# A decoder block in fp32 on one Trainium2 core: output projection as seven block products, second feed-forward begun by a hand order with six chunks

## The chip, the cores and the metric

The kernel runs on one core of a Trainium2 chip. The time is the device time of one execution in microseconds (us); the kernel before took 1117.46 us, the median of 3 runs (1116.97 to 1117.51). Engines are named as in the profile: PE (TensorE), DVE (VectorE), ACT (ScalarE), POOL (GpSimd) and SP (SyncE, which here only issues transfers).

## What is computed

One decoder block on 512 tokens with 1024 features: feed-forward, token mixing, feed-forward, each between two norms. The change touches the end of the token mixing (the output projection, its norm and residual) and the first chunks of the second feed-forward. The reference, cut to that:

```python
def hybrid_mixer(u, ...):
    ...
    merged = jax.nn.sigmoid(g_lru) * (y_lru @ w_proj_lru) + jax.nn.sigmoid(g_attn) * (y_attn @ w_proj_attn)
    return merged @ w_out

def reference(x, ...):
    ...
        m = hybrid_mixer(rms_norm(h, mix_pre_g[l]), ...)
        h = h + rms_norm(m, mix_post_g[l])
        f = swiglu(rms_norm(h, ffn2_pre_g[l]), ffn2_w_gu[l], ffn2_w_down[l])
        h = h + MACARON_SCALE * rms_norm(f, ffn2_post_g[l])
```

`swiglu` projects to 2 x 2816 columns, multiplies silu of one half with the other, and projects back.

## The kernel before

**Products.** Every fp32 product is made of three matmuls (`mm3`, L157 to L160) on operands that are split into a high and a low part: high by high, high by low, low by high. A weight half of 128 x 1024 numbers is loaded by SP (`wload`, L102, tile `wraw`), cast to its high part on ACT (`wround`, L112, tile `w`), and its low part is the difference, on DVE (`wsplit`, L120). `worder` lists all weight halves in the order in which they are used; `wget` hands out the next one and keeps the split some halves ahead.

**Stages.** In the order of time: the first feed-forward; the mixing's input projections; the left-gate stage (tiles `glg`, `glp`, eight chunks, 527 to 639 us in the trace), into which the attention of the last head groups is woven (`at20b`, `at30b` and so on: scores of group 2 and 3, block 0); the right-gate stage (`gag`, `gap`, 640 to 727 us), which ends with the merged features `mg`, split into high and low; the output projection (`token_out`, L449, tiles `woo`); and the second feed-forward: `first_four` (L238, four column chunks `f2f`, each in two halves of 256 tokens), four more whole chunks (`f2g`), and then the rest in pairs as block products (`paired`, tiles `f2X` and others).

**Attention's queries.** A group's rotated queries pass through memory: SP stores them (`q_halves`, L960) and reads them back in another layout in four transfers (`qt`, L965). `at20b` is the first user of `qt2`, `at30b` of `qt3`. The sums of attention's blocks (`at20s` and others) run on POOL.

**Output projection.** For each of 4 token tiles and 2 column halves a bank adds up 8 chunks. Seven of the chunks are held back, so that a tile is finished at a time. Its epilogue (`boundary`, L481) follows at once on the other engines: squares on ACT (`half`, L502), gains on DVE (L506), an inverse root on POOL (L203), the residual (L529), a second norm (L534 to L542, tile `b2un`). Then PE transposes the tile (`b2ntp`, L218), and ACT and DVE split it (`u3h` L222, `u3l` L223).

**What sets the order.** In all these stages a scheduler decides the order of instructions on each engine from the program's order and its own costs; blocks under `manual_schedule` keep the order that is written. Each engine then runs its list in order. Transfers issued by SP go to one queue (q1 in the profile), those by POOL to another (q0). The kernel before already has sums of weights in memory for the down projections: SP copies (`wsum`, L393), and POOL adds to the copy (an accumulating transfer, L395).

Of the kernel before, what the change touches and what calls it, by code (L numbers as in the profile page):

```python
# [8 lines left out]
F32 = mybir.dt.float32  # L9
# [33 lines left out]
def hybrid_block_kernel(ctx, tc, x, xt, g1, w_first, gains, gu1, gs1, dn1, w_x, w_gate, w_q, w_k, w_v, w_gl, w_ga, w_pl, w_pa,  # L43
# [12 lines left out]
    def bank(name):  # L56
        return psum.tile([P, 512], F32, name=name, tag="bank")
# [154 lines left out]
    def to_features(un, t, u, name, raw=None):  # L212
        keep = []
        for half in range(2):
            b = bank(f"{name}tp{t}{half}")
            for i in range(4):
                k = 4 * half + i
                PE.transpose(out=b[:, i * P:(i + 1) * P], in_=un[:, k * P:(k + 1) * P], identity=ident)  # L218
            bv = b.rearrange("p (k t) -> p k t", k=4)
            ts_ = slice(t * P, (t + 1) * P)  # L220
            uh, ul = u[0][half][:, :, ts_], u[1][half][:, :, ts_]
            A.copy(uh, bv)  # L222
            V.tensor_tensor(out=ul, in0=bv, in1=uh.bitcast(F32), op=ALU.subtract)  # L223
            if raw is not None:
                keep.append((raw[half][:, :, ts_], bv))
        for z, bv in keep:
            A.copy(z, bv)

    def feat_chunk(b, w, u, tok):
        wh, wl = w  # L230
# [7 lines left out]
    def first_four(u, name, done):  # L238
# [14 lines left out]
    def gate_up(u, name, first, fast, then, rs=None):  # L253
        ps = []

        def slot(j):
# [21 lines left out]
            if i % 2 == 1:  # L278
                tail(i // 2, bs[i - 1], b)

        first(u, f"{name}f", done)
        run = paired(fast, name, slot, then(ps))
        for j in range(2, JSTD[name]):
            if j == JSTD[name] - 1:
                next(run)
# [13 lines left out]
    def paired(fast, name, slot, then):  # L299
# [78 lines left out]

        for k in range(3):
            load(k)  # L380
        sums(0)
        parts(0, 1)
        parts(0, 2)
# [62 lines left out]
            add(n - 1, 21)  # L446
            finish(n - 1)

    def token_out(chunk, n, finish, name, tail_n):  # L449
        half, epilogue, _ = finish  # L450
        banks = {}

        def block(t, c, w, i):
            ph, pl = chunks[c]
            ts_ = slice(t * P, (t + 1) * P)
            if (t, i) not in banks:
                banks[t, i] = bank(f"{name}o{t}{i}")
            ns = slice(i * 512, (i + 1) * 512)
            mm3(banks[t, i], ph[:, c % 4, ts_], pl[:, c % 4, ts_], w[0][:, ns], w[1][:, ns], c == 0, c == n - 1)

        chunks = {}
        tail = []
        for c in range(n):
            w = wget()
            chunks[c] = chunk(c)
            if c < n - tail_n:
                for t in range(NT):
                    for i in range(2):
                        block(t, c, w, i)
                tick()  # L470
            else:
                tail.append((c, w))
        for t in range(NT):
            for i in range(2):
                for c, w in tail:
                    block(t, c, w, i)
            for i in range(2):
                half(t, i, banks[t, i])
            start(epilogue(t))
            tick()  # L480

    def boundary(src, dst, g_post, g_pre, u, scale, name, raw=None, then=None):
        rhs = []

        def residual():
# [4 lines left out]
                rhs.append(rh)  # L490

        cols = (slice(0, 512), slice(512, 1024))
        sq, parts, late = {}, {}, {}

        def half(t, i, z, sign=1.0, o=None):
            if t not in sq:
                sq[t], parts[t] = sm(f"{name}ps{t}", 2), [None, None]
# [4 lines left out]
            A.activation(t4(f"{name}sq{t}{i}")[:, :512], z, AF.Square, scale=1.0 / 32.0, accum_out=sq[t][:, i:i + 1])  # L502
            parts[t][i] = o

            def gain():
                V.scalar_tensor_tensor(out=o, in0=z, scalar=sign * scale, in1=g_post[:, cols[i]], op0=ALU.mult,  # L506
                                       op1=ALU.mult)

            if i == 0:
                gain()  # L510
            else:
                late[t] = gain

        def inverse(ms, z):
            me = sm(f"{name}{z}e")
# [3 lines left out]
        def epilogue(t):  # L519
# [4 lines left out]
            late[t]()  # L524
            yield
            if g_pre is not None:
                ms, un = sm(f"{name}ms{t}", 2), t4(f"{name}un{t}")
# [14 lines left out]
                V.scalar_tensor_tensor(out=un[:, cols[i]], in0=h[:, cols[i]], scalar=r, in1=g_pre[:, cols[i]],  # L542
                                       op0=ALU.mult, op1=ALU.mult)
            yield FEATURE_LAG[name][t]
            to_features(un, t, u, f"{name}n", raw)
            if then is not None and t == NT - 1:
                start(then())

# [554 lines left out]
    start(split_y(y1, "ya1"))  # L1103
    while live:
        tick()
    mg = []
    for c in range(KD):
        s, b = sig_gate(c, ya, "ga")
        if c % 4 == 0:
            mg.append((b8(f"mgh{c}", [P, 4, T], F32R), b8(f"mgl{c}", [P, 4, T], F32R)))  # L1110
        V.scalar_tensor_tensor(out=s, in0=s, scalar=1.0, in1=b, op0=ALU.add, op1=ALU.mult)
        V.tensor_tensor(out=s, in0=s, in1=m1[c // 4][:, c % 4, :], op=ALU.add)
# [6 lines left out]
    u3 = new_u("u3")  # L1119
    hs2 = [dram.tile([P, D], F32, name=f"h2_spill{t}") for t in range(NT)]  # L1120
    raw3 = [b8(f"u3r{i}", [P, 4, T]) for i in range(2)]
    mv3 = {}
    finish = boundary(hs, hs2, g_post, g_pre, u3, 1.0, "b2", raw3, lambda: moving(raw3, "u3", mv3))
    for _ in range(2):
        finish[2]()
# [11 lines left out]
def _layout(inputs):  # L1137
# [90 lines left out]
```

## Time and profile before

| | us |
|---|---|
| median of 3 runs | 1117.46 |
| the profiled execution | 1116.89 |
| its span, first to last instruction | 1115.1 |
| output projection, first `woo` to first `f2f` | 726.95 to 773.64 |
| `f2f` and `f2g`, to the first `f2X` | 773.64 to 821.08 |
| DMA share 520 to 540, 540 to 560, 560 to 580 us | 0.70, 0.70, 0.16 |

The span is from the first to the last instruction of the profiled execution; the time beside it also holds what lies around it. In a timeline's row stand the start, the duration, engine, line and operation, output and inputs, and in brackets how long the engine was idle before it and what ended that. In the rows of a window stand the busy time of PE, of its weight load, of DVE, ACT and POOL, then the clock granted to PE, the busy share of the 16 DMA engines and GB/s. The granted clock is 0.999 of full speed over the span.

### The profile page before, as it was taken

The page shows a single profiled execution, that of the slowest core. Times are in us where ns is not written, and L with a number is a line of the kernel's source. Part 1 is how long each engine was busy: PE and PEld are TensorE (multiplying, and loading weights), DVE is VectorE, ACT ScalarE, POOL GpSimd, SP SyncE. Part 2 cuts the span into 40 slices and gives each one's busy share as a digit, 9 for nine tenths or more (in the row PEclk, how much of TensorE's full clock was granted, in tenths as well). Part 3 has the DMA queues.
Part 4 walks back from the last instruction along what each step waited for, and adds up shares of the span by engine and source line. Part 5 has one row for each costly group of instructions (what it writes and reads, how often), then busy time and mean ns, then how long its engine had stood idle before and what let it go on. Part 6 is the DMA issues. An engine that isn't in the chain of part 4 may idle for free.

```text
span 1115.1 us, 16841 instructions
## 1 busy us (share of the span) xinstructions
PE 1102.8 (99%) x6558; PEld 982.3 (88%) x6558; DVE 883.2 (79%) x1341; ACT 592.2 (53%) x991; POOL 77.8 (7%) x82
## 2 busy tenths in 40 slices
PE   9999999999999999999999999999999999999997
PEld 7889999988878888888888888888999999998885
DVE  6998898889898788988766462546858889988896
ACT  7445555465664758576546351436435455456662
POOL 1000010000000001122112000001000000000000
PEclk9999999999999999999999999999999999999999
DMA  9239999664677172612812340623348999455483
GB/s 364 78 124 259 305 286 293 205 226 125 220 262 270 58 208 99 185 57 83 257 58 95 114 170 20 208 94 132 114 115 262 300 281 302 121 165 191 153 274 114
DMA packets 53279, 202.07 MB, mean 181 GB/s; under 512 B 6352, under 2 KB 6480, under 8 KB 48464
## 3 DMA queue, kind: packets, MB, share of 16 engines
q1 hardware_dynamic: 45424, 163.77, 43.5%
q0 software_dynamic: 3456, 23.07, 10.6%
q10 hardware_dynamic: 4320, 14.16, 3.5%
q8 instruction: 51, 0.84, 0.3%
q14 instruction: 28, 0.23, 0.1%
HBM read 189.44 MB, written 57.67 MB: 222 GB/s over the span
## 4 chain that ended last, share of the span: by engine, by line
PE 91%; DVE 6%; DMA 1%; issue 1%; ACT 1%; POOL 0%; SPq 0%; DVEq 0%; POOLq 0%; ACTq 0%
PE f2X L160 5%; PE f2X L159 5%; PE f2X L158 5%; PE f1X L160 4%; PE f1X L158 4%; PE f1X L159 4%; PE f2Q L160 2%; PE f2Q L159 2%; PE f2Q L158 2%; PE f1Q L160 2%; PE f1Q L158 2%; PE f1Q L159 2%; PE f1f L790 2%; DVE w L120 2%; PE glg L158 1%; PE f1g L158 1%
## 5 line engine op out<-in xcount | busy, mean ns | idle before, releaser
L120 DVE TENSOR_TENSOR w<-wraw,w 128x1024 fp32r<-128x1024 f32 x168 | 196.7, 1192 | 28.6 <-ACT w L112 28.3
L112 ACT CAST w<-wraw 128x1024 fp32r<-128x1024 f32 x168 | 163.0, 1011 | 29.9 <-issue 9.1
L160 PE MATMUL f1X<-u1m,f1W 128*128 128x256 f32 x256 | 72.5, 283 | 0.1
L159 PE MATMUL f1X<-u1m,f1W 128*128 128x256 f32 x256 | 72.4, 283 | 0.0
L158 PE MATMUL f1X<-u1m,f1W 128*128 128x256 f32 x256 | 72.4, 283 | 0.0
L160 PEld LDWEIGHTS f1X<-u1m,f1W 128*128 128x128 f32 x256 | 49.1, 192 | 0.3 <-DVE f1W L329 0.3
L158 PEld LDWEIGHTS f1X<-u1m,f1W 128*128 128x128 f32 x256 | 49.1, 192 | 0.1
L159 PEld LDWEIGHTS f1X<-u1m,f1W 128*128 128x128 f32 x256 | 49.1, 192 | 0.1
L160 PE MATMUL f2X<-u3m,f2W 128*128 128x256 f32 x144 | 40.9, 284 | 0.1
L159 PE MATMUL f2X<-u3l,f2W 128*128 128x256 f32 x144 | 40.8, 283 | 0.0
L160 PE MATMUL f2X<-u3h,f2W 128*128 128x256 f32 x144 | 40.8, 283 | 0.0
L158 PE MATMUL f2Q<-u3m,f2W 128*128 128x256 f32 x144 | 40.8, 283 | 0.0
L159 PE MATMUL f2Q<-u3m,f2W 128*128 128x256 f32 x144 | 40.8, 283 | 0.0
L160 PE MATMUL f2Q<-u3m,f2W 128*128 128x256 f32 x144 | 40.8, 283 | 0.0
L158 PE MATMUL f2X<-u3m,f2W 128*128 128x256 f32 x144 | 40.7, 283 | 0.0
L159 PE MATMUL f2X<-u3m,f2W 128*128 128x256 f32 x144 | 40.7, 283 | 0.0
L158 PE MATMUL f2X<-u3h,f2W 128*128 128x256 f32 x144 | 40.7, 283 | 0.0
L158 PE MATMUL f1Q<-u1m,f1W 128*128 128x256 f32 x128 | 36.2, 283 | 0.0
L159 PE MATMUL f1Q<-u1m,f1W 128*128 128x256 f32 x128 | 36.2, 283 | 0.0
L160 PE MATMUL f1Q<-u1m,f1W 128*128 128x256 f32 x128 | 36.2, 283 | 0.0
L159 PE MATMUL f1X<-w,f1y 128*128 128x512 f32 x88 | 34.5, 392 | 0.4 <-DVE w L120 0.4
L159 PE MATMUL f2X<-w,f2y 128*128 128x512 f32 x88 | 34.5, 392 | 0.4 <-DVE w L120 0.4
(829 smaller groups left out, 3740.5 us busy)
## 6 DMA issues: line engine op xcount, KB each, us to landing
wraw<-wsum SPq DMA_DIRECT2D x40, 512.0 KB, 4.4
wsum<-in_dn_dram SPq DMA_DIRECT2D x16, 1024.0 KB, 10.0
wraw<-in_dn_dram SPq DMA_DIRECT2D x30, 512.0 KB, 4.7
f2L<-in_gs_dram SPq DMA_DIRECT2D x18, 512.0 KB, 4.9
f2R<-in_gs_dram SPq DMA_DIRECT2D x18, 512.0 KB, 5.0
wraw<-in_gu_dram SPq DMA_DIRECT2D x16, 512.0 KB, 5.8
f1L<-in_gs_dram SPq DMA_DIRECT2D x16, 512.0 KB, 5.2
f1R<-in_gs_dram SPq DMA_DIRECT2D x16, 512.0 KB, 6.2
```

What stands on the lines that cost most here:

```text
L112: A.copy(w[:, 0, :], raws[n])
L120: V.tensor_tensor(out=w[:, 1, :], in0=raws[n], in1=w[:, 0, :].bitcast(F32), op=ALU.subtract)
L158: PE.matmul(o, lhsT=ah, rhs=bh, start=start, stop=False, skip_group_check=reopen)
L159: PE.matmul(o, lhsT=ah, rhs=bl, start=False, stop=False, skip_group_check=reopen)
L160: PE.matmul(o, lhsT=al, rhs=bh, start=False, stop=stop, skip_group_check=reopen)
L790: PE.matmul(bs[i], lhsT=lw[:, i * P:(i + 1) * P], rhs=rx, start=k == 0 and n == 0, stop=k == KD - 1 and n == 2)
```

## The change

The merged features and the output weights are each cut in 2 x 2 blocks, and the projection is made of seven products of block sums in place of eight products of blocks. The sums of weight blocks `t1` to `t4` are made in memory (`osums`): SP copies a 1 MB block, POOL adds another by an accumulating transfer. Block sums of the features are made on DVE and split on ACT and DVE. The products' banks are combined through copies in SBUF (`snap` on ACT, `plus` on DVE). The whole stage and the second feed-forward's first part, now with six chunks in halves (`first_six`) and two whole ones, stand under `manual_schedule`. The copies of the transposed tile for the paired products are put off.

```diff
-FEATURE_LAG = {"b1": (7, 9, 7, 3), "b2": (3, 3, 3, 3)}
+FEATURE_LAG = {"b1": (7, 9, 7, 3), "b2": (1, 1, 5, 6)}
...
+    osums = dram.tile([P, 4, 4 * 512], F32, name="osums")
+    osum = [osums[:, i, :] for i in range(4)]
...
-            worder += [w_o[c] for c in range(8)]
+            t1, t2_, t3, t4_ = osum
+            for w in (w_o[0], w_o[1], t2_, t1, w_o[3], t3, t4_):
+                worder += [w[:, i:i + 1024] for i in (0, 1024)]
...
+    def first_six(u, name, done, early):
+        first = []
+        for i in range(6):
+            first.append((wnow(), bank(f"{name}{i}")))
+            if i < 5:
+                wsplit(wpos[0] + 1)
+            feat_chunk(first[i][1], first[i][0], u, HALVES[0])
+            tick()
+        for i, (w, b) in enumerate(first):
+            if i == 2:
+                early()
+            if i >= 4:
+                wsplit(wpos[0] + i - 3)
+            feat_chunk(b, w, u, HALVES[1])
+            tick()
+            done(i, b)
...
+    oplan = ((0, 2, 0), (2, 3, 2), (1, 3, None), (3, 1, None))
     for c in range(KD):
         gate_chunk(c)
...
+        if 2 <= c < 6:
+            with tc.issue_after(wdma[wpos[0]].ins):
+                SP.dma_start(osum[oplan[c - 2][0]], w_o[oplan[c - 2][1]])
...
-        mh, ml = mg[-1]
-        A.mul(mh[:, c % 4, :], s, 0.5)
-        V.scalar_tensor_tensor(out=ml[:, c % 4, :], in0=s, scalar=0.5, in1=mh[:, c % 4, :].bitcast(F32),
-                               op0=ALU.mult, op1=ALU.subtract)
+        V.tensor_tensor(out=mg[c // 4][:, c % 4, :], in0=s, in1=m1[c // 4][:, c % 4, :], op=ALU.add)
+        if c % 2 == 0 and c < 6:
+            for o, _, b in (oplan[:2], oplan[2:3], oplan[3:])[c // 2]:
+                G.dma_start(osum[o], osum[o // 2] if b is None else w_o[b], accum_op=ALU.add)
...
-    token_out(lambda c: mg[c // 4], KD, finish, "wo", TAILS)
+        product(1, first_sums, next_sum)
+        snap("a", X)
+        for _ in range(2):
+            residual()
+        product(2, lambda: oop_split(6, S[2], -1.0), lambda: osum_tile("os4", S[2], a12, ALU.subtract, S[2]))
+        wround(wpos[0] + 3)
+        for t in range(2):
+            plus("a", Y, t)
+        product(6, lambda: oop_split(5, S[1]), lambda: oop_split(3, S[2]))
+        snap("u", X)
+        product(5, halves, lambda: oop_split(4, a22))
+        snap("q", Q)
+        product(3, lambda: None, lambda: wsplit(wpos[0] + 4))
+        for t in range(2):
+            plus("u", Q, t)
+            half(t, 1, sn["u"][t], -1.0)
...
+        w = [wnow() for _ in range(2)]
+        for t in range(2):
+            for k in range(4):
+                unit(7, k, w[k // 2], (t,))
+            plus("q", X, t)
...
+        for k in range(4):
+            unit(4, k, w[k // 2], (0,))
+        half(2, 0, X[0])
...
-    gate_up(u3, "f2", first_four, lambda: (gs2, blocks(u3, mv3)), begin(dn_run, "f2"))
+    with tc.manual_schedule():
+        token_out()
+        gate_up(u3, "f2", first_six, lambda: (gs2, blocks(u3, mv3)), begin(dn_run, "f2"), j0=3)
...
-    a["w_o"] = c(f["w_out"].reshape(KD, P, D))
+    w = f["w_out"].reshape(2, 4, P, 2, 512)
+    a["w_o"] = c(np.stack([w[j, :, :, i].transpose(1, 0, 2).reshape(P, 2048) for i in range(2) for j in range(2)]))
```

Three places show what the change moves. The first is SP's list of transfers in the left-gate stage: `q_halves` is the store of a query group, `qt` its read-back (`qt2`, then `qt3`), `wraw` a weight half. Before:

```order
L960 DMA q_halves_5378<-q2st 128x2048
L102 DMA wraw_5460<-in_w_pl_dram 128x1024
L102 DMA wraw_5520<-in_w_gl_dram 128x1024
L965 DMA qt_5436<-q_halves_5378 32x4x512 x4
L960 DMA q_halves_5515<-q3st 128x2048
L965 DMA qt_5555<-q_halves_5515 32x4x512 x4
L102 DMA wraw_5593<-in_w_pl_dram 128x1024
```

and of the change:

```order
L966 DMA q_halves_5379<-q2st 128x2048
L105 DMA wraw_5461<-in_w_pl_dram 128x1024
L105 DMA wraw_5521<-in_w_gl_dram 128x1024
L1107 DMA osums<-in_w_o_dram 128x2048
L971 DMA qt_5437<-q_halves_5379 32x4x512 x4
L966 DMA q_halves_5516<-q3st 128x2048
L105 DMA wraw_5594<-in_w_pl_dram 128x1024
L105 DMA wraw_5634<-in_w_gl_dram 128x1024
L1107 DMA osums<-in_w_o_dram 128x2048
L971 DMA qt_5556<-q_halves_5516 32x4x512 x4
```

A copy of 1 MB stands ahead of the first read-back, and two weight halves and the second copy ahead of the second read-back.

The second is POOL's list in the same stage; `q3m` belongs to the rotation of the last query group. Before, no transfer stands there:

```order
L936 TENSOR_TENSOR q3m_5441<-q3m_5441,q3m_5444 128x512
L997 TENSOR_TENSOR at20s<-at20s,at20ss 128x512
L997 TENSOR_TENSOR at30s<-at30s,at30ss 128x512
L997 TENSOR_TENSOR at21s<-at21s,at21ss 128x1024
L997 TENSOR_TENSOR at31s<-at31s,at31ss 128x1024
```

and of the change:

```order
L942 TENSOR_TENSOR q3m_5442<-q3m_5442,q3m_5445 128x512
L1147 DMA osums<-in_w_o_dram 128x2048
L1003 TENSOR_TENSOR at20s<-at20s,at20ss 128x512
L1147 DMA osums<-in_w_o_dram 128x2048
L1003 TENSOR_TENSOR at30s<-at30s,at30ss 128x512
L1003 TENSOR_TENSOR at21s<-at21s,at21ss 128x1024
L1147 DMA osums<-osums 128x2048
L1003 TENSOR_TENSOR at31s<-at31s,at31ss 128x1024
L1147 DMA osums<-osums 128x2048
```

The accumulating transfers, written in the loop of the right-gate stage, stand among the attention sums of the left-gate stage.

The third is DVE in the projection, ahead of the first tile's epilogue (L506 or L509 is a gain, L516 or L519 the start of an inverse root, L529 or L533 the residual). Before:

```order
L120 TENSOR_TENSOR w_7053<-wraw_7041,w_7053 128x1024
L120 TENSOR_TENSOR w_7058<-wraw_7046,w_7058 128x1024
L1112 TENSOR_TENSOR gas_6938<-gas_6938,m_6073 128x512
L1115 SCALAR_TENSOR_TENSOR mgl_6771<-gas_6938,mgh_6770 128x512
L506 SCALAR_TENSOR_TENSOR b2rh_6987<-woo_6996,g_b_6974 128x512
L516 TENSOR_SCALAR b2p0e<-b2ps_7105 128x1
L506 SCALAR_TENSOR_TENSOR b2rh_6987<-woo_7000,g_b_6974 128x512
L529 SCALAR_TENSOR_TENSOR b2rh_6987<-b2rh_6987,b2p0r 128x512 x2
L516 TENSOR_SCALAR b2n0e<-b2ms_7116 128x1
L542 SCALAR_TENSOR_TENSOR b2un_7117<-b2rh_6987,b2n0r,g_b_6974 128x512 x2
```

and of the change (`oy` is a split of a feature block sum, `wou` a combined bank):

```order
L1129 TENSOR_TENSOR oy_7153<-mg_6448,oy_7153 128x1024
L123 TENSOR_TENSOR w_7172<-wraw_7102,w_7172 128x1024
L123 TENSOR_TENSOR w_7189<-wraw_7126,w_7189 128x1024
L123 TENSOR_TENSOR w_7194<-wraw_7151,w_7194 128x1024
L123 TENSOR_TENSOR w_7199<-wraw_7175,w_7199 128x1024
L1187 TENSOR_TENSOR wou_7119<-woQ_6989,wou_7119 128x512
L1187 TENSOR_TENSOR wou_7120<-woQ_6990,wou_7120 128x512
L519 TENSOR_SCALAR b2p0e<-b2ps_7128 128x1
L509 SCALAR_TENSOR_TENSOR b2rh_7035<-wou_7119,g_b_6976 128x512
L519 TENSOR_SCALAR b2p1e<-b2ps_7132 128x1
L509 SCALAR_TENSOR_TENSOR b2rh_7037<-wou_7120,g_b_6976 128x512
L1187 TENSOR_TENSOR woq_7168<-woX_6985,woq_7168 128x512
```

The splits of weight halves that stood ahead of the projection's last merge now stand among the combinations, four of them ahead of the first `wou`.

More of the change, by code (lines that the diff above doesn't have):

```diff
@@ L225, in to_features @@
                 keep.append((raw[half][:, :, ts_], bv))
-        for z, bv in keep:
-            A.copy(z, bv)
+        return [lambda z=z, bv=bv: A.copy(z, bv) for z, bv in keep]
     def feat_chunk(b, w, u, tok):
@@ L279, in done, with early @@
                 tail(i // 2, bs[i - 1], b)
-        first(u, f"{name}f", done)
         run = paired(fast, name, slot, then(ps))
-        for j in range(2, JSTD[name]):
+        loads = []
+        def early():
+            if not loads:
+                loads.append(next(run))
+        first(u, f"{name}f", done, early)
+        for j in range(j0, JSTD[name]):
             if j == JSTD[name] - 1:
+                early()
                 next(run)
@@ L380, in paired @@
             load(k)
+        yield
         sums(0)
@@ L447, in paired, with boundary @@
             finish(n - 1)
[L449 to L482, printed above, removed]
+    def boundary(src, dst, g_post, g_pre, u, scale, name, raw=None, then=None, unit=1.0):
         rhs = []
@@ L492, in boundary, with half @@
         cols = (slice(0, 512), slice(512, 1024))
-        sq, parts, late = {}, {}, {}
-        def half(t, i, z, sign=1.0, o=None):
+        sq, parts, late, copies = {}, {}, {}, []
+        def half(t, i, z, sign=1.0, o=None, wait=False):
             if t not in sq:
-                sq[t], parts[t] = sm(f"{name}ps{t}", 2), [None, None]
+                sq[t], parts[t], late[t] = sm(f"{name}ps{t}", 2), [None, None], []
+                wait = wait or i == 1
+            else:
+                wait = True
             if o is None:
@@ L523, in epilogue @@
             r = inverse(sq[t], f"p{t}")
-            late[t]()
+            for gain in late[t]:
+                gain()
             yield
@@ L544, in epilogue @@
             yield FEATURE_LAG[name][t]
-            to_features(un, t, u, f"{name}n", raw)
+            copies.extend(to_features(un, t, u, f"{name}n", raw))
+            while t > 0 and copies:
+                copies.pop(0)()
             if then is not None and t == NT - 1:
@@ L1105, in hybrid_block_kernel, with oop_new, oop_split @@
         tick()
-    mg = []
+    mg = [b8(f"mg{i}", [P, 4, T]) for i in range(2)]
+    lo_, hi_ = slice(0, 256), slice(256, 512)
+    a11, a21, a12, a22 = (mg[i][:, :, tok] for i in range(2) for tok in (lo_, hi_))
+    oop = {}
+    def oop_new(i):
+        oop[i] = b8(f"oy{i}", [P, 2, 4, 256], F32R)
+        return oop[i]
+    def oop_split(i, z, sign=1.0, ks=slice(0, 4)):
+        o = oop[i] if i in oop else oop_new(i)
+        if sign == 1.0:
+            A.copy(o[:, 0, ks], z[:, ks])
+            V.tensor_tensor(out=o[:, 1, ks], in0=z[:, ks], in1=o[:, 0, ks].bitcast(F32), op=ALU.subtract)
+        else:
+            A.activation(o[:, 0, ks], z[:, ks], AF.Copy, scale=sign)
+            V.scalar_tensor_tensor(out=o[:, 1, ks], in0=z[:, ks], scalar=sign, in1=o[:, 0, ks].bitcast(F32),
+                                   op0=ALU.mult, op1=ALU.subtract)
@@ L1118, in hybrid_block_kernel @@
+        if c == 4:
+            oop_split(1, a11)
+        if c == 5:
+            oop_split(7, osum_tile("os3", a11, a21, ALU.subtract))
+            oop_split(2, a12, ks=slice(0, 2))
     g_post, g_pre = gain_pair(3, 2, "g_b2")
-    u3 = new_u("u3")
     hs2 = [dram.tile([P, D], F32, name=f"h2_spill{t}") for t in range(NT)]
-    raw3 = [b8(f"u3r{i}", [P, 4, T]) for i in range(2)]
-    mv3 = {}
-    finish = boundary(hs, hs2, g_post, g_pre, u3, 1.0, "b2", raw3, lambda: moving(raw3, "u3", mv3))
@@ L1124, in hybrid_block_kernel, with token_out, unit, product @@
-    for _ in range(2):
-        finish[2]()
-    token_out(lambda c: mg[c // 4], KD, finish, "wo", TAILS)
+    raw3, u3, mv3 = [], [], {}
+    def token_out():
+        X, Y, Q = ([bank(f"wo{z}{t}") for t in range(2)] for z in "XYQ")
+        dst = {1: X, 2: Y, 6: X, 5: Q, 3: Q, 7: X, 4: X}
+        half, epilogue, residual = boundary(hs, hs2, g_post, g_pre, u3, 1.0, "b2", raw3,
+                                            lambda: moving(raw3, "u3", mv3), 0.5)
+        def unit(i, k, w, tiles):
+            y, n = oop[i], k % 2 * 512
+            for t in tiles:
+                ts_ = slice(t * P, (t + 1) * P)
+                mm3(dst[i][t], y[:, 0, k, ts_], y[:, 1, k, ts_], w[0][:, n:n + 512], w[1][:, n:n + 512],
+                    k == 0 and i in (1, 2, 5), k == 3, True)
+        def product(i, *prep):
+            for n in range(2):
+                w = wget()
+                if n < len(prep):
+                    prep[n]()
+                for k in (2 * n, 2 * n + 1):
+                    unit(i, k, w, range(2))
+        sn = {}
+        def snap(key, z):
+            sn[key] = [t2(f"wo{key}{t}") for t in range(2)]
+            for t in range(2):
+                A.copy(sn[key][t], z[t])
+        def plus(key, z, t):
+            V.tensor_tensor(out=sn[key][t], in0=z[t], in1=sn[key][t], op=ALU.add)
+        S = {}
+        def first_sums():
+            oop_split(2, a12, ks=slice(2, 4))
+            S[1] = osum_tile("os1", a22, a21, ALU.subtract)
+        def next_sum():
+            S[2] = osum_tile("os2", S[1], a11, ALU.add)
+        def halves():
+            for t in range(2):
+                half(t, 0, sn["a"][t])
+        product(1, first_sums, next_sum)
[11 more added lines that the diff above has]
+        product(3, lambda: None, lambda: wsplit(wpos[0] + 4))
+        for t in range(2):
+            plus("u", Q, t)
+            half(t, 1, sn["u"][t], -1.0)
+        wround(wpos[0] + 6)
+        u3.extend(new_u("u3"))
+        raw3.extend(b8(f"u3r{i}", [P, 4, T]) for i in range(2))
+        e = [epilogue(t) for t in range(NT)]
+        for t in range(2):
+            next(e[t])
+        w = [wnow() for _ in range(2)]
+        for t in range(2):
+            for k in range(4):
+                unit(7, k, w[k // 2], (t,))
+            plus("q", X, t)
+            half(2 + t, 1, sn["q"][t], -1.0, sn["q"][t], True)
+            if t == 0:
+                next(e[0])
+                next(e[1])
+        w = [wnow() for _ in range(2)]
+        next(e[0])
+        next(e[1])
+        wsplit(wpos[0] + 1)
+        next(e[0])
+        next(e[1])
+        wround(wpos[0] + 4)
+        for k in range(4):
+            unit(4, k, w[k // 2], (0,))
+        half(2, 0, X[0])
+        for n in range(2):
+            for k in (2 * n, 2 * n + 1):
+                unit(4, k, w[n], (1,))
+            if n == 1:
+                half(3, 0, X[1])
+            next(e[n], None)
+        wsplit(wpos[0] + 2)
+        next(e[2])
+        next(e[3])
+        wsplit(wpos[0] + 3)
+        next(e[2])
+        next(e[3])
+        wsplit(wpos[0] + 4)
+        next(e[2])
+        next(e[3])
+        wround(wpos[0] + 5)
+        for t in (2, 3):
+            live.append([e[t], next(e[t])])
+            wsplit(wpos[0] + 5)
```

30 lines of the change are left out of this document (18 added, 12 removed).

## The prediction

> **What bounds the kernel now.** I read the busy times first, then the chain that ended last, then what TensorE waited for.
>
> ```profile
> span 1115.1 us, 16841 instructions
> PE 1102.8 (99%) x6558; PEld 982.3 (88%) x6558; DVE 883.2 (79%) x1341; ACT 592.2 (53%) x991; POOL 77.8 (7%) x82
> PE 91%; DVE 6%; DMA 1%; issue 1%; ACT 1%; POOL 0%; SPq 0%; DVEq 0%; POOLq 0%; ACTq 0%
> ```
>
> TensorE is busy for 99% of the span and carries 91% of the chain. So the kernel is a queue of matmuls in a fixed order: a matmul that goes saves its pitch, and any wait at the head of this queue is paid in full, since nothing behind it has slack to win it back. The list of PE's waits shows how few there are:
>
> ```profile
> PE f2f L158 <- ACT u3h L222: 1.2, 1, 1.2
> PE at10b L982 <- DMA qt<-q_halves: 0.7, 1, 0.7
> PE f2f L159 <- DVE u3l L223: 0.5, 1, 0.5
> ```
>
> Two of them, 1.2 + 0.5 = 1.7 us, lie in the stretch that the change rewrites. The third is a read-back of q (`qt`) that reached its first user 0.7 us late; it shows that these transfers are already timed closely.
>
> **The change: matmuls.** The timeline of PE gives the pitch, which counts and not the duration (the ends overlap), and the groups of the stretch 727 to 822 us give the counts.
>
> ```profile
> L158 PE MATMUL woo<-w,mgh 128*128 128x512 f32 x64 | 25.0, 390 | 0.0
> L158 PE MATMUL f2f<-u3h,w 128*128 128x256 f32 x64 | 18.4, 287 | 1.2 <-ACT u3h L222 1.2
> L158 PE MATMUL f2g<-u3h,w 128*128 128x512 f32 x32 | 12.5, 389 | 0.0
> ...
> 726.95 0.39 PE L158 MATMUL woo<-w,mgh 128*128 128x512 f32 x1
> 727.17 0.39 PE L159 MATMUL woo<-w,mgh 128*128 128x512 f32 x1
> ...
> 775.87 0.28 PE L158 MATMUL f2f<-u3h,w 128*128 128x256 f32 x1
> 775.99 0.28 PE L159 MATMUL f2f<-u3l,w 128*128 128x256 f32 x1
> ...
> 821.08 0.28 PE L158 MATMUL f2X<-u3h,f2W 128*128 128x256 f32 x1
> ```
>
> A 128x512 matmul starts every 0.227 us, a 128x256 one every 0.12 us. Each product of the kernel is three matmuls (high by high, high by low, low by high). The projection (`woo`) has 3 x 64 = 192 of them; seven block products of 4 channel chunks, 2 token tiles and 3 matmuls make 168. So 24 matmuls go: 24 x 0.227 = **5.4 us less**. The first feed-forward chunks in halves (`f2f`) were 192 matmuls for four chunks and become 288 for six, 96 x 0.12 = 11.5 us more; the whole chunks (`f2g`) lose two of four, 48 x 0.227 = 10.9 us less. Together **0.6 us more**.
>
> **The change: waits around these matmuls.** The products need more from the other engines: copies of sums out of PSUM, splits of operand sums into high and low, and fourteen instead of eight weight halves to cast and subtract. These are the durations; the last two rows are the ends of one tile's old epilogue.
>
> ```profile
> L120 DVE TENSOR_TENSOR w<-wraw,w 128x1024 fp32r<-128x1024 f32 x19 | 22.3, 1220 | 4.1 <-ACT w L112 4.1
> L506 DVE SCALAR_TENSOR_TENSOR b2rh<-woo,g_b 128x512 f32<-128x512 f32 x8 | 5.5, 683 | 6.0 <-ACT b2sq L502 6.0
> ...
> L112 ACT CAST w<-wraw 128x1024 fp32r<-128x1024 f32 x17 | 17.1, 1052 | 5.6 <-issue 3.5 <-PE gag L159 1.3 <-PE gag L160 0.7
> L502 ACT ACTIVATE b2sq<-woo 128x512 f32<-128x512 f32 x8 | 4.8, 599 | 20.3 <-PE woo L160 20.3
> ...
> 742.17 0.60 ACT L502 ACTIVATE b2sq<-woo 128x512 f32<-128x512 f32 x1 [2.71 <-PE woo L160]
> ...
> 746.87 1.41 DVE L542 SCALAR_TENSOR_TENSOR b2un<-b2rh,b2n0r,g_b 128x512 f32<-128x512 f32 x2 [0.67 <-POOL b2n0r L203]
> ```
>
> An epilogue took 742.2 to 748.3, 6.1 us from the last square to the normalised tile, and each of its steps waits for the one before. In the new hand order I followed five places where PE can reach work too early.
> 1. Product 3 reuses the bank that ACT copies out behind casts of 1.05 us: I estimate 0.3 to 0.6 us.
> 2. Tile 0's transposes stand after product 7 and half of product 4: 36 matmuls, 8.2 us after product 3's end. Its epilogue takes 6.1 us alone, and now shares DVE and ACT with tile 1 (each step doubles, about 0.7 us for each of the two PSUM additions and again for the shared gains and squares), after four splits of 1.2 us that stand ahead of it on DVE: about 9.3 us. The wait is about 1.2 us.
> 3. The first `f2f` matmul follows the transposes of tiles 0 and 1 at once, where before a whole product lay between for these two tiles. The old 1.2 us wait for tile 2's copy is of this kind: about 1.3 us.
> 4. Chunks three and four of `f2f` need weights whose splits stand behind both tiles' `u3l` on DVE: one split late, about 1.2 us.
> 5. The second token half waits for the last tile's `u3l`: about 0.9 us.
>
> These make about 5.0 us against the 1.7 us of now, so **3.3 us more**. From the lowest case, no wait at all, to doubled waits this term lies between -1.7 and +8. I take 5.0 since each is a row's duration or the difference of two chains of rows. The stage alone then gives -5.4 + 0.6 + 3.3 = **-1.5 us**. The extra casts, subtractions and six weight loads ahead of the stage cost nothing: in the right-gate stage DVE is busy for 41.5 of 87 us and the transfers for 0.39 of the time. If that cover were gone, six more pairs would cost 6 x 1.2 = 7 us.
>
> ```profile
> 526.00:531.00 5.00, 5.00 (x28) 4.22 (x27) 5.00 (x7) 2.04 (x4) 0.00 (x0) 1.00 0.62 215
> 531.00:542.00 11.00, 11.00 (x54) 9.22 (x53) 9.01 (x13) 6.45 (x10) 2.53 (x2) 1.00 0.98 282
> 542.00:548.00 6.00, 6.00 (x32) 5.04 (x32) 5.39 (x14) 2.69 (x4) 0.00 (x0) 1.00 0.53 128
> ...
> 560.00:580.00 20.00, 20.00 (x101) 16.86 (x101) 12.53 (x26) 10.13 (x26) 4.74 (x3) 1.00 0.16 54
> ...
> 640.00:727.00 87.00, 87.00 (x386) 72.06 (x385) 41.51 (x47) 33.00 (x43) 0.00 (x0) 1.00 0.39 134
> ```
>
> **The change: eight new transfers of 1 MB.** In the windows' rows above, the last two numbers are the share of the DMA engines' time and GB/s. From 531 to 542 us that share is 0.98: there nothing can be hidden. Just there the order of SP puts the first copy into `osums` ahead of the four loads of `qt2`, and the second copy with two weight loads ahead of the four of `qt3`. Two accumulating transfers on POOL's queue follow, each when its copy has landed. The page's queues give the price of a megabyte.
>
> ```profile
> q1 hardware_dynamic: 45424, 163.77, 43.5%
> q0 software_dynamic: 3456, 23.07, 10.6%
> ```
>
> 0.435 x 1115.1 / 163.77 = 2.96 us of all sixteen engines for a MB of SP's and ACT's queue, 0.106 x 1115.1 / 23.07 = 5.1 us for one of POOL's. The next rows are the issues on SP, from narrow windows the time to landing of the last `qt2`, of the store before `qt3`, and of the last `qt3`, and the first use of each on PE.
>
> ```profile
> 531.83 1.79 SPq L965 DMA_DIRECT2D qt<-q_halves  x4
> 537.91 0.34 SPq L960 DMA_DIRECT2D q_halves<-q3st  x1
> 543.62 1.73 SPq L965 DMA_DIRECT2D qt<-q_halves  x4
> ...
> qt<-q_halves SPq DMA_DIRECT2D x2, 256.0 KB, 7.8
> ...
> q_halves<-q3st SPq DMA_DIRECT2D x1, 1024.0 KB, 5.6
> ...
> qt<-q_halves SPq DMA_DIRECT2D x1, 256.0 KB, 6.2
> ...
> L982 PEld LDWEIGHTS at20b<-kp,qt x8: 188/192/192, 542.3 to 543.2; 128*128 128x128 f32 x8
> ...
> L982 PEld LDWEIGHTS at30b<-kp,qt x8: 188/192/192, 555.0 to 555.9; 128*128 128x128 f32 x8
> ```
>
> `qt2`: issued until 533.3 and landed at 533.3 + 7.8 = 541.1, used at 542.3: 1.2 us to spare. Behind the copy it lands 3.0 us later, so PE stands for **1.8 us** at `at20b`. Below, a copy that found free engines before 531 (share 0.62) would leave nothing; above, an accumulation beside the load adds up to 5.1.
>
> `qt3` can be issued only when the store of its data has landed, 537.9 + 5.6 = 543.5, and came in at about 544.9 + 6.2 = 551.1, used at 555.0: 3.9 us to spare, and 5.7 after the first stall. The first copy moves the store by 3.0. Two weight loads and the second copy, 2 MB or 5.9 us, now stand ahead of `qt3`: 551.1 + 8.9 = 560.0, **3.2 us** after 556.8. If they run entirely while SP waits for the store (share 0.53 from 542 to 548), this is nothing. Then the accumulations: whether a load beside one is slowed is seen where before has both.
>
> ```profile
> 185.86 0.81 POOL L395 DMA_DIRECT2D wsum<-wsum  x1 [5.10 <-DMA wsum<-in_dn_dram]
> ...
> f1L<-in_gs_dram SPq DMA_DIRECT2D x1, 512.0 KB, 9.3
> f1R<-in_gs_dram SPq DMA_DIRECT2D x1, 512.0 KB, 10.6
> ...
> f1L<-in_gs_dram SPq DMA_DIRECT2D x16, 512.0 KB, 5.2
> f1R<-in_gs_dram SPq DMA_DIRECT2D x16, 512.0 KB, 6.2
> ```
>
> The loads issued within a microsecond or so of that accumulation landed after 9.3 and 10.6 us; all sixteen have medians of 5.2 and 6.2. So a load beside an accumulation comes 4 us late. [...]
>
> The third and fourth copies fall where the share is 0.16, and `osums` is first read by the weight loads of the projection, some 100 us later: nothing. POOL itself now waits for a copy ahead of each accumulation, with the attention blocks' sums (`at20s`, `at30s`, `at21s`) queued behind it. POOL is busy for 4.7 of the 20 us from 560 to 580, so it has room: I count nothing, and up to 2 us if a copy lands so late that the sums' readers wait.
>
> **Sum.** Stalls 1.8 + 3.2 + 3.0 = 8.0; the projection's stage -1.5; together +6.5 us. The profiled execution took 1116.89 us (span 1115.1), 0.57 under the median of the runs shown, 1117.46; the new time will be a median too, so 1117.46 + 6.5 = **1123.9 us**.
>
> **Rivals.**
> - *The transfers are hidden* (the other side). One mechanism: at the SP queue of 530 to 556 us the copies run in the gaps that the shares 0.62 and 0.53 leave. It decides at `qt2`'s landing before 542.3 and `qt3`'s before 555. Then only the stage's -1.5 is left, 1116.0; and if its waits are also gone (-5.4 + 0.6 - 1.7 = -6.5) 1111.0. Against it stands the 0.98.
> - *Only the first load is late*: 1.8 - 1.5, 1117.8. For it speaks that `qt3` has 3.9 us to spare and that SP's wait for the store leaves its queue idle.
> - *DVE becomes the bound in the projection*: four splits in a row and both tiles' epilogues double the five waits to 10 us, and transfers cost little: -5.4 + 0.6 + 8.3 + 1.8 = +5.3, 1122.8. For it: DVE's order is now by hand with no slack; against: DVE stood idle for 6.0 us ahead of its gain operations (L506), room that the new order can fill.
>
> **How the numbers follow.** Forecast (both loads late, 5 to 11 us, so 1121 to 1127): 0.53. Hidden: 0.20. First load only: 0.17. DVE: 0.10. The range reaches from 1113.5, the middle of the hidden case, to 1128.5, the upper bounds of the stalls (11) with 1.5 us of worse waits. A measurement can tell about 0.2% (2.2 us) from no change. Faster than 1115.2: two thirds of the hidden case, 0.14. Slower than 1119.7: forecast, DVE and a little of the others, 0.65. Same: 0.21. All of the forecast's own range is slower.
>
> **What would show it.** Right: PE waits at `at20b` and `at30b` for `qt`, of some 2 and 6 us, and the projection to the first `f2X` takes 1.5 us less than the present 94.1 us (726.95 to 821.08). Wrong: PE without a wait in the left-gate stage (the copies were hidden), landing times of `qt` as now, or waits of over 7 us between the first `woX` and the first `f2X`.

## The result and the profile after

| | before | after |
|---|---|---|
| median, us | 1117.46 (1116.97 to 1117.51, 5 runs) | 1122.35 (1120.90 to 1122.81, 5 runs) |
| profiled execution, its span, us | 1116.89, 1115.1 | 1122.35, 1120.6 |

The ratio is 1.0045, with a 95% interval of 1.0034 to 1.0056: the change makes the kernel 4.9 us slower. The page of the changed kernel shows that TensorE is busy no longer than before (1102.9 against 1102.8 us), and that each queue moves more:

```profile
span 1120.6 us, 16935 instructions
PE 1102.9 (98%) x6582; PEld 982.5 (88%) x6582; DVE 899.9 (80%) x1357; ACT 602.3 (54%) x1003; POOL 83.0 (7%) x86
q1 hardware_dynamic: 46864, 171.11, 45.0%
q0 software_dynamic: 4032, 27.26, 12.3%
```

So 5.5 us of span were added with hardly any more busy time. The list of PE's waits names one long wait that was not in the old list, the one at `at30b`; the short ones at `f2f` lie in the rewritten stage:

```profile
PE at30b L988 <- DMA qt<-q_halves: 4.7, 1, 4.7
...
PE at10b L988 <- DMA qt<-q_halves: 1.3, 1, 1.3
PE f2f L168 <- DVE u3l L232: 0.7, 2, 0.3
PE f2f L167 <- ACT u3h L231: 0.7, 2, 0.4
PE f2f L169 <- DVE w L123: 0.5, 2, 0.3
```

Four rows of PE's timeline cut the time into stretches: the first matmuls of `at20b`, `at30b`, the projection and `f2X`.

```profile
543.32 0.41 PE L988 MATMUL at20b<-kp,qt 128*128 128x128 f32 x2
...
560.92 1.94 PE L988 MATMUL at30b<-kp,qt 128*128 128x128 f32 x8 [4.65 <-DMA qt<-q_halves]
...
735.33 0.39 PE L167 MATMUL woX<-w,oy 128*128 128x512 f32 x1
...
826.69 0.28 PE L167 MATMUL f2X<-u3h,f2W 128*128 128x256 f32 x1
```

The kernel before has its first `at20b` at 542.49 and its first `at30b` at 555.23, without an idle time ahead of either:

```profile
542.49 0.89 PE L982 MATMUL at20b<-kp,qt 128*128 128x128 f32 x7
...
555.23 1.00 PE L982 MATMUL at30b<-kp,qt 128*128 128x128 f32 x8
```

The other two stand at 726.95 and 821.08. From `at20b` to `at30b` 12.74 us have become 17.60, **4.9 more**. From `at30b` to the projection 171.72 have become 174.41, **2.7 more**, though no matmul there is new. From the projection to `f2X` 94.13 have become 91.37, **2.8 less**. At `at20b` the changed kernel is 0.8 us late. It was 0.7 us late already when SP issued the store of `qt2`'s data (527.96 against 527.22), before the first new transfer at 530.73. This start differs from kernel to kernel below by up to 1.9 us, so the stretches, not the times of day, are compared.

Where the 2.7 us come from is seen in the windows: behind the wait the granted clock (the third number from the end) is 0.50 for six microseconds, while TensorE has work.

```profile
540.00:556.00 16.00, 16.00 (x75) 13.04 (x74) 10.63 (x23) 8.09 (x18) 1.32 (x2) 1.00 1.04 315
556.00:560.00 4.00, 0.27 (x2) 0.00 (x0) 0.69 (x1) 2.18 (x4) 0.84 (x1) 0.96 1.09 211
560.00:566.00 6.00, 5.08 (x20) 4.82 (x21) 3.63 (x22) 1.94 (x10) 0.00 (x0) 0.50 1.05 303
566.00:568.00 2.00, 2.00 (x9) 1.57 (x9) 0.09 (x2) 1.94 (x8) 1.04 (x1) 0.87 1.05 287
```

From 560.9, where TensorE goes on, to 566, a clock of 0.50 costs about half of the 5.1 us, 2.5, and 0.13 x 2 = 0.3 more follow. Together, an estimate from these rows, they are the 2.7 us to within 0.1.

The DMA rows of narrow windows give the time from issue to landing: of the last `qt2`, of the store that `qt3` waits for, of POOL's first accumulation, of the second copy, and of the last `qt3`. A row with x2 has the middle value of the last two.

```profile
qt<-q_halves SPq DMA_DIRECT2D x2, 256.0 KB, 9.1
...
q_halves<-q3st SPq DMA_DIRECT2D x1, 1024.0 KB, 8.1
...
osums<-in_w_o_dram POOLq DMA_DIRECT2D x1, 1024.0 KB, 12.2
...
osums<-in_w_o_dram SPq DMA_DIRECT2D x1, 1024.0 KB, 15.4
...
qt<-q_halves SPq DMA_DIRECT2D x2, 256.0 KB, 12.2
```

The store went from 5.6 to 8.1 us, the read-back from 6.2 to over 12, and the second copy, issued ahead of it beside the accumulation, took 15.4.

### The profile page after: what moved, and what is told of

It is laid out like the page before. It is cut to its first block, busy times and chain, and to the rows that moved or that the text cites. A ratio compares the mean times of both kernels' runs of the same rounds, so it can differ in the third digit from the quotient of the medians.

```text
span 1120.6 us, 16935 instructions
## 1 busy us (share of the span) xinstructions
PE 1102.9 (98%) x6582; PEld 982.5 (88%) x6582; DVE 899.9 (80%) x1357; ACT 602.3 (54%) x1003; POOL 83.0 (7%) x86
## 5 line engine op out<-in xcount | busy, mean ns | idle before, releaser
L123 DVE TENSOR_TENSOR w<-wraw,w 128x1024 fp32r<-128x1024 f32 x174 | 204.2, 1194 | 24.7 <-ACT w L115 24.4
L115 ACT CAST w<-wraw 128x1024 fp32r<-128x1024 f32 x174 | 169.0, 1012 | 29.4 <-PE glp L169 7.4
L1143 DVE SCALAR_TENSOR_TENSOR gas<-gas,gap 128x512 f32<-128x512 f32 x8 | 5.5, 688 | 45.2 <-PE gap L169 45.2
```

The source lines that it names most:

```text
L115: A.copy(w[:, 0, :], raws[n])
L123: V.tensor_tensor(out=w[:, 1, :], in0=raws[n], in1=w[:, 0, :].bitcast(F32), op=ALU.subtract)
```

## The experiments

The table has for each kernel its median, the ratio to the kernel before with its interval, and from the profiled execution three stretches on TensorE: `at20b` to `at30b`, `at20b` to the projection, and the projection to `f2X`. One profiled execution lies far from its median: that of "POOL copies plainly" took 1116.72 us, 2.7 us less, and its stretches are those of this execution.

| kernel | median, us | ratio, interval | at20b to at30b | at20b to projection | projection to f2X |
|---|---|---|---|---|---|
| before | 1117.46 | | 12.74 | 184.45 | 94.13 |
| the change | 1122.35 | 1.0045 (1.0034, 1.0056) | 17.60 | 192.00 | 91.37 |
| copies later | 1114.35 | 0.9974 (0.9964, 0.9984) | 12.74 | 184.45 | 91.33 |
| the same again | 1113.73 | 0.9972 (0.9961, 0.9983) | 12.74 | 184.45 | 91.36 |
| before plus sums | 1125.62 | 1.0072 (1.0055, 1.0088) | 17.47 | 192.19 | 94.13 |
| POOL copies plainly | 1119.44 | 1.0024 (1.0014, 1.0033) | 14.99 | 186.77 | 91.33 |
| second copy later | 1119.96 | 1.0031 (1.0018, 1.0043) | 15.53 | 188.94 | 91.33 |
| both of these | 1114.50 | 0.9977 (0.9967, 0.9987) | 13.73 | 185.52 | 91.35 |
| wait filled | 1118.88 | 1.0018 (1.0009, 1.0028) | 17.31 | 189.10 | 91.33 |
| second later, filled | 1118.23 | 1.0018 (1.0007, 1.0029) | 15.99 | 187.77 | 91.36 |
| later, four chunks | 1115.88 | 0.9989 (0.9979, 0.9998) | 12.74 | 184.45 | 93.79 |
| later, two splits on POOL | 1116.90 | 1.0002 (0.9993, 1.0011) | 12.74 | 184.45 | 94.75 |

**Are the transfers the loss?** The copies were put two chunks later, behind `qt3`:

```diff
-        if 2 <= c < 6:
+        if 4 <= c < 8:
             with tc.issue_after(wdma[wpos[0]].ins):
-                SP.dma_start(osum[oplan[c - 2][0]], w_o[oplan[c - 2][1]])
+                SP.dma_start(osum[oplan[c - 4][0]], w_o[oplan[c - 4][1]])
```

> The four copies into osums stand two chunks later in the left-gate stage, so that the first comes behind the last read-back qt3 and its two weight loads; nothing else of the change is moved, and TensorE's order is the same. Theory A (all of the loss is the read-back qt3 behind the new transfers, and what its wait brings with it): no wait at at30b, the clock stays at 1.00, the first woX at 727 to 728 us instead of 735.3, and the time falls by 7.5 to 8.5 us to 1114 to 1115, below the kernel before by the 2.8 us that the projection's stage has won. Rival (the new transfers cost as much wherever they stand in this stage, since the engines' time is what is short): some other wait takes their place, and the time stays above 1119.

SP now reads `qt3` back first. The first copy comes behind it, and so do the two weight loads that stood ahead of it in the change:

```profile
543.90 1.74 SPq L971 DMA_DIRECT2D qt<-q_halves  x4
545.68 0.43 SPq L105 DMA_DIRECT2D wraw<-in_w_pl_dram  x1
546.22 0.36 SPq L105 DMA_DIRECT2D wraw<-in_w_gl_dram  x1
...
547.82 0.50 SPq L1107 DMA_DIRECT2D osums<-in_w_o_dram  x1
```

The stretch to the projection is the old one to the hundredth, 184.45 us, so the same eight transfers cost nothing when they stand there. What is left is the projection's 2.8 us, and the kernel is faster than both others: 1114.35 us. The rival, that the engines' time is short wherever the copies stand, falls.

The other way round, the transfers were added to the kernel before, whose projection makes nothing of them:

```diff
+        if 2 <= c < 6:
+            with tc.issue_after(wdma[wpos[0]].ins):
+                SP.dma_start(osum[oplan[c - 2][0]], flat[oplan[c - 2][1]])
...
+        if c % 2 == 0 and c < 6:
+            for o, _, z in (oplan[:2], oplan[2:3], oplan[3:])[c // 2]:
+                G.dma_start(osum[o], osum[o // 2] if z is None else flat[z], accum_op=ALU.add)
```

> The kernel before with the eight transfers into osums at the places that they have in the change (the sums are made of the old weight blocks and used by nothing); the projection and the feed-forward are the old ones, and the order on SP and POOL in the left-gate stage is that of the change. Theory (the transfers alone are the loss): the stretch from at20b to the first matmul of the projection grows from 184.5 to about 192 us as in the changed kernel (7.5 us more), time 1124 to 1125.5, which is more than the changed kernel by the 2.8 us that its projection wins. Rival (the loss needs the change's other edits in this stage, or the projection's stage wins nothing): below 1122.4.

```profile
560.73 1.51 PE L984 MATMUL at30b<-kp,qt 128*128 128x128 f32 x6 [4.53 <-DMA qt<-q_halves]
```

The wait is there again, the stretch is 192.19 us, and the time 1125.62, 0.1 us over the range that was expected. With the two kernels the change is taken apart: 7.6 to 7.7 us for the transfers where they stand, 2.8 us won by the new stage.

**Which transfer delays `qt3`?** First POOL's transfers were made plain copies of the same size, which leaves the order on all engines as it was (the sums of weights are not formed):

```diff
-                G.dma_start(osum[o], osum[o // 2] if b is None else w_o[b], accum_op=ALU.add)
+                G.dma_start(osum[o], osum[o // 2] if b is None else w_o[b])
```

> POOL's four transfers into osums copy in place of adding, so the weight sums are not formed; same sizes, and the same order on every engine. A plain transfer of 1 MB should hold the DMA engines about half as long as an accumulating one (2.96 against 5.1 us a MB by the two queues). Theory B (sharing with POOL's queue is a large part of the delay of qt3): the last qt3 lands 2 to 3 us earlier, the wait at at30b falls from 4.7 to about 2 to 3 us and the clock may not fall; time 1117 to 1119. Theory A (what stands ahead on SP's own queue sets it): the wait stays within 0.7 us of 4.7 and the time within 1 us of the changed kernel's 1122.4.

```profile
557.96 1.08 PE L988 MATMUL at30b<-kp,qt 128*128 128x128 f32 x8 [2.05 <-DMA qt<-q_halves]
```

The wait fell by 2.6 us, as theory B had it; the median of 1119.44 is 0.4 us over its range, and the last section says what is likely behind it. So accumulating in place of copying is a part of the delay, though it stands on another queue than `qt3`. Whether the two meet at the DMA engines or at the memory was not taken apart. Then the second copy alone was put behind `qt3`:

```diff
-        if 2 <= c < 6:
+        n = {2: 0, 4: 1, 5: 2, 6: 3}.get(c)
+        if n is not None:
             with tc.issue_after(wdma[wpos[0]].ins):
-                SP.dma_start(osum[oplan[c - 2][0]], w_o[oplan[c - 2][1]])
+                SP.dma_start(osum[oplan[n][0]], w_o[oplan[n][1]])
```

> Only the copies from the second on stand later (chunks 4, 5, 6); the first copy, its accumulation and the two weight loads stay ahead of qt3, the second copy no longer does. Theory A: 1 MB less ahead of qt3, which beside an accumulation took about 4.5 us of the 9.1 us for these 2 MB: qt3 lands 3 to 4.5 us earlier, the wait at at30b falls to 0.2 to 1.7 us, the clock stays at 1.00, time 1114.5 to 1116.5. Theory B: the first accumulation is unchanged and holds the store and qt3 as before: a wait over 2.5 us, time over 1117.5.

```profile
558.30 1.08 PE L988 MATMUL at30b<-kp,qt 128*128 128x128 f32 x8 [2.63 <-DMA qt<-q_halves]
...
558.00:560.00 2.00, 1.70 (x15) 1.73 (x16) 1.02 (x7) 0.00 (x0) 0.00 (x0) 1.00 1.05 424
560.00:562.00 2.00, 2.00 (x9) 1.62 (x8) 1.93 (x11) 1.62 (x8) 0.00 (x0) 0.54 1.00 420
562.00:564.00 2.00, 2.00 (x7) 1.63 (x6) 0.60 (x6) 1.64 (x8) 1.04 (x1) 0.61 0.62 240
```

Here theory A as I had put it failed: the wait fell by 2.0 us, not by 3 to 4.5, and wait and time lie where theory B had them. The clock fell to 0.54 after a wait of 2.6 us, which I had not expected. So I asked whether the two shares add:

> Both partial edits together: the second copy behind qt3, and POOL's transfers into osums copy in place of adding (the weight sums are not formed). Each alone brought the last qt3 2.1 and 2.6 us closer to at20b, of the 4.7 us that at30b waited. If the shares add (the queue ahead of qt3 and the accumulation's hold on the engines are separate terms): 4.7 us less, so a wait of 0 to 0.5 us, no fall of the clock, and a time of 1114 to 1115. Rival (they are one and the same term, what is removed twice counts once): a wait of about 2 us as with each alone, time 1116.5 or more.

```profile
PE at30b L988 <- DMA qt<-q_halves: 0.8, 1, 0.8
```

The last `qt3` lands 17.46 us after the first `at20b` in the change, 14.86 with plain copies, 15.39 with the second copy later, and 13.60 with both: 2.6 and 2.1 apart, 3.9 together, where 4.7 would be the full sum. They add in the main: two terms, the queue ahead and the sharing beside it, each of about 2 to 3 us. In the kernel before the last `qt3` lands 8.60 us after `at20b`, so 5.0 us are left with both removed: the first copy, the two weight loads and POOL's plain copy are still there. The 0.8 us of wait lies a little outside what was expected, the time within it.

**Is the slow stretch behind the wait the wait's doing?** Eighteen matmuls that need nothing late were put ahead of `at30b`:

```diff
+            if nm == "at30" and half == 0:
+                for _ in range(18):
+                    PE.matmul(b, lhsT=kp[0][:, 0, 0, 0:P], rhs=kp[1][:, 0, 0, :], start=True, stop=True)
```

> Eighteen additional matmuls of 128x512 into the bank of at30b stand on TensorE ahead of it; they need nothing from the late loads, and at30b overwrites what they leave. They take 18 x 0.227 = 4.1 us of the 4.7 us that TensorE waits there. Clock theory (after the wait TensorE runs for some 6 us at half its clock, and that is the other 2.7 us of the loss): the wait shrinks to about 0.6 us, the clock stays at 1.00, and with 4.1 us more of work the time falls by 2.5 to 2.9 us, to 1119.5 to 1120. Rival (the slow stretch after the wait has another cause, as late operands): the time stays at 1122 to 1123.

```profile
L986 PE MATMUL at30b<-kp,kp x18: 388/389/389, 555.1 to 559.0; 128*128 128x512 f32 x18
...
L991 PE MATMUL at30b<-kp,qt x8: 272/276/299, 559.7 to 560.5; 128*128 128x128 f32 x8
```

`at30b` comes nearly as late as in the change (17.31 us after `at20b`), but its matmuls take 276 ns and not 415, and the stretch to the projection loses 2.9 us. With more work the median is 3.5 us lower, 0.6 us below the range that was expected. So the clock is the second part of the loss, 2.7 of the 7.6 us, and the rival of late operands falls. The same with nine matmuls in the kernel with the second copy later:

> The kernel with the second copy later, whose profile shows a wait of 2.6 us at at30b and then the clock at 0.54 and 0.61 in two windows of 2 us, with nine additional matmuls of 128x512 ahead of at30b (2.0 us of work that needs nothing late). Theory (a wait of 2.6 us is already enough to bring the clock down, and what follows costs more than half as much again): the wait falls to about 0.6 us, the clock stays at 1.00, and the time falls by 1.5 to 2 us from 1119.96 to 1118 to 1118.5, though work was added. Rival (the clock's fall there was an accident of the profiled run and is rare): the time stays at 1119.5 to 1120.5.

```profile
558.00:560.00 2.00, 1.15 (x10) 1.18 (x11) 0.71 (x4) 2.00 (x4) 0.00 (x0) 1.00 1.03 410
560.00:562.00 2.00, 2.00 (x14) 1.78 (x14) 1.93 (x13) 1.17 (x7) 0.00 (x0) 1.00 1.04 436
```

A wait of 1.0 us was left, the clock stayed at 1.00, and the median fell by 1.7 us, into the expected range. The intervals of the two kernels in the table overlap, so the difference of the medians is weak evidence by itself; the traces show the clock's fall without the filling, behind 2.63 us of wait, and none with it, behind 1.0.

**What is the projection's stage made of?** On the kernel with the later copies, the feed-forward begins with four chunks, and the transposes of tiles 2 and 3 come two chunks earlier, to stay ahead of the second half:

```diff
-FEATURE_LAG = {"b1": (7, 9, 7, 3), "b2": (1, 1, 5, 6)}
+FEATURE_LAG = {"b1": (7, 9, 7, 3), "b2": (1, 1, 3, 4)}
...
-        for i in range(6):
+        for i in range(4):
...
-            if i < 5:
+            if i < 3:
...
-            if i >= 4:
-                wsplit(wpos[0] + i - 3)
+            if i >= 2:
+                wsplit(wpos[0] + i - 1)
...
-        gate_up(u3, "f2", first_six, lambda: (gs2, blocks(u3, mv3)), begin(dn_run, "f2"), j0=3)
+        gate_up(u3, "f2", first_six, lambda: (gs2, blocks(u3, mv3)), begin(dn_run, "f2"), j0=2)
```

> The kernel with the later copies, but the second feed-forward begins with four chunks in halves in place of six (and the lags of the last two tiles' transposes are cut from 5 and 6 chunks to 3 and 4, to stay ahead of the second half). Theory (the six chunks are cover: the 48 additional 128x256 matmuls ahead of the second half take 5.8 us in which DVE and ACT finish tiles 2 and 3): 0.6 us of matmuls are saved, but the wait for the last tiles grows from 1.1 by 3 to 6 us, part of it as DVE has two weight splits less to do ahead of them; time 2.5 to 5.5 us above the later copies' 1114.35, 1116.8 to 1119.9. Rival (the second half would be ready anyway): 0.6 us less, 1113.7.

```profile
780.06 1.75 PE L227 MATMUL b2ntp<-ident,b2un 128*128 128x128 f32 x8 [2.21 <-DVE b2un L546]
...
780.00:785.00 5.00, 4.91 (x28) 4.73 (x29) 4.23 (x6) 2.35 (x4) 0.00 (x0) 0.66 0.35 105
```

The stage is 2.5 us longer in the trace, and the median 1.5 us higher: less than the 2.5 to 5.5 I had expected. Now tile 2's transposes wait 2.2 us for DVE, and the clock is 0.66 in the window behind it. So the two added chunks are cover, of about 2 us.

Last, the two waits for weight splits in `f2f`: two low parts are made on POOL.

```diff
-    def wsplit(upto):
+    def wsplit(upto, low=None):
...
-            V.tensor_tensor(out=w[:, 1, :], in0=raws[n], in1=w[:, 0, :].bitcast(F32),
+            (low or V).tensor_tensor(out=w[:, 1, :], in0=raws[n], in1=w[:, 0, :].bitcast(F32),
...
-        wsplit(wpos[0] + 3)
+        wsplit(wpos[0] + 3, G)
...
-        wsplit(wpos[0] + 4)
+        wsplit(wpos[0] + 4, G)
```

> On the kernel with the later copies, the low parts of two weight halves for the first feed-forward chunks (the second and third that the hand order splits after product 4) are formed on POOL in place of DVE. In the later copies' trace f2f waits 0.5 us at 778.9 and 0.5 us at 782.3 for splits that DVE ends there, behind the epilogues of tiles 2 and 3. Theory (DVE's order sets these two waits): both go, and with them 1.0 us, to 1113.3; the wait at the second half (1.1 us) stays, as it is the way from the transposes through ACT and DVE. Rival (POOL's 128x1024 subtraction is so slow, or so disturbs DVE, that the inverse roots behind it on POOL come late): no gain or a loss of 1 to 3 us.

> The kernel with the later copies once more, on the chip and beside the runs of the one with two splits on POOL: 1114 to 1115 by all theories.

```profile
781.42 0.39 PE L167 MATMUL f2f<-u3h,w 128*128 128x256 f32 x1 [0.60 <-ACT w L115]
...
783.19 0.58 PE L169 MATMUL f2f<-u3h,w 128*128 128x256 f32 x1 [1.27 <-DVE w L123]
...
784.00:786.00 2.00, 2.00 (x11) 2.00 (x11) 1.59 (x2) 0.00 (x0) 0.00 (x0) 0.50 0.00 0
...
772.60 5.20 POOL L123 TENSOR_TENSOR w<-wraw,w 128x1024 fp32r<-128x1024 f32 x2
...
772.73 2.80 DVE L533 SCALAR_TENSOR_TENSOR b2rh<-b2rh,b2p2r 128x512 f32<-128x512 f32 x1
775.46 2.89 DVE L533 SCALAR_TENSOR_TENSOR b2rh<-woq,b2p2r,b2rh 128x512 f32<-128x512 f32 x1
778.27 0.74 DVE L533 SCALAR_TENSOR_TENSOR b2rh<-b2rh,b2p3r 128x512 f32<-128x512 f32 x1
```

No gain: the kernel is 3.2 us slower than the one with the later copies on the same chip. Each of DVE's residual operations that met one of POOL's subtractions took 2.80 or 2.89 us in place of 0.74, and DVE was later than with the splits of its own: from its first gain (L509) of tile 2 to that tile's normalised form it took 11.8 us, with the later copies 9.8. The stage is 3.4 us longer. About 1.9 us of that are longer waits for the weights. The other 1.5 us are the clock again: behind the waits of 0.60 and 1.27 us it fell to 0.50, and fifteen matmul starts took 3.3 us where the pitch makes 1.8.

## Why the prediction was right, point by point

The forecast was 1123.9 us, from stalls of 8.0 and a gain of 1.5; measured were 7.6 (184.45 to 192.00) and 2.8, and 1122.35 us. The place and the mechanism of the main loss held: `qt3` came late behind the new transfers, and nothing hid it. The terms did not all have their sizes, one of them came to almost nothing, and one was missing. That the sum came within 1.6 us is in part luck. Of the three signs named in advance the wait at `at30b` came, the wait of some 2 us at `at20b` did not, and the stage became shorter by 2.8 us in place of 1.5.

- **The projection's matmuls, -5.4, and the chunks', +0.6.** The counts held: PE has 6582 instructions for 6558, which is 24 less, 96 more and 48 less. That 94.13 us became 91.37 fits them with the next point.
- **The five waits, 3.3 us more.** Right in kind, too large. The matmuls of the stage at their pitch make 192 x 0.227 + 192 x 0.12 + 96 x 0.227 = 88.4 us before and 168 x 0.227 + 288 x 0.12 + 48 x 0.227 = 83.6 now; what is left of 94.13 and 91.37, waits and transposes, is 5.7 and 7.8: 2.1 us more, not 3.3, so the stage won 2.8 and not 1.5. Two errors made it. The old waits were taken from PE's list (1.7 us) and set against chains that were worked out in full; counted by starts that come later than the pitch, they are 2.3 us. By the same count the five places have about 0.3, 0.5, 1.3, 1.1 and 1.0 us, so tile 0's transposes, sized at 1.2 us, are the one that was far too large. The 0.2 us that are left to the 2.1 were not placed.
- **`at20b`, 1.8 us.** This step failed. The last `qt2` landed 0.1 us ahead of its first matmul, against 542.49 - 541.1 = 1.4 us in the kernel before: the copy made it 1.3 us later, not 3.0. It landed just in time; in three of the kernels above with the first copy in the same place PE did stand, for 0.2 to 0.4 us. My step took the share of 0.98 for engines with no room. They moved 282 GB/s in that window of the kernel before and 315 in the same window of the changed one, 0.83 us later by its start. So a part of the copy did fit in; why the rest delayed `qt2` so little was not taken apart.

```profile
531.83:542.83 11.00, 11.00 (x55) 9.18 (x54) 8.72 (x12) 5.28 (x8) 3.42 (x3) 1.00 1.02 315
```

- **`at30b`, 6.2 us.** Measured 4.9. The last `qt3` came 8.9 us later against the first `at20b`; I had 8.9 us from the queue and 3.0 from sharing on top, less the 1.8 by which `at20b` itself was to be late, 10.1 in all. No run shows the 3.0 us that the sum of the stalls has for the accumulations; in their place the runs showed 2.6 us for accumulating in place of copying, and 2.1 for the second copy. Nor did accumulating act where I had put it, on the store of q3: that took 8.0 us with plain copies against 8.1, and the read-back's last two 10.0 against 12.2. What the first copy and the two weight loads add was not taken apart.
- **The clock.** Missing from the sum: a term of 2.7 us, more than half of the 4.65 us of wait that bring it. By luck it made up for most of the term at `at20b`, which came to 0.1, and of what `at30b` was short of its 6.2.
- **The third and fourth copies and POOL's sums, nothing.** This held. PE's list has no new wait between `at30b` and the projection, and with the wait filled this stretch takes 171.78 us, as against 171.72 in the kernel before.

The rival in which the transfers are hidden is what the later copies show: 1114.35 against the 1116.0 worked out for it, since the stage wins more than was counted. The rival in which only the first load is late is the reverse of what came. That of DVE as the bound falls too: its five waits were to be 10 us and are about 4.

## What to carry to other kernels

Transfers whose sums nobody read for 100 us cost 7.6 us here by their place in a queue: look what the next small transfer behind one is for, and how long its reader can wait. Two chunks later they were free. Price TensorE's waits with the clock behind them, and fill them with any work that is ready: here the clock fell to 0.50 behind 4.65 us and to 0.54 behind 2.63 us, and stayed at 1.00 where the wait was filled down to 0.3 and 1.0 us. Do not divide a busy engine's work with another one before the trace has shown that both can run side by side: here DVE's operations of 0.74 us took 2.80 and 2.89 beside POOL's.

## What the runs showed of the hardware that was not expected

- The clock fell behind an idle time of 2.63 us with the second copy later (0.54 and 0.61 in the two windows from 560 to 564 us), of 2.21 us in the four-chunk kernel (0.66 from 780 to 785), and with two splits on POOL behind 0.60 and 1.27 us that ended 1.8 us apart (0.50 from 784 to 786). It did not in the profiled execution with plain copies, behind a wait of 2.05 us (1.00 from 556 to 570). That one took 1116.72 us at a granted clock of 0.999, while nine other runs of the kernel took 1118.8 to 1123.2 at 0.995 to 0.998. That the clock fell behind the wait in those is likely, and was not seen: they have no trace, and the kernel before ran beside them at 0.998 to 1.000, so only the four at 0.995 to 0.997 stand apart. What sets when the clock falls was not taken apart.
- Beside POOL's two subtractions in 5.20 us, two DVE operations took 2.80 and 2.89 us; the same operations take 0.74 us each with the later copies, where DVE makes these splits. Why they took longer was not taken apart.
